# A 16-token opening, early branch constants, branch A's sums on DVE and a memory projection in single banks, in a one-core hybrid mixer layer

## The chip, the cores and the metric

The kernel is one program on 1 core of a Trainium2 chip. The core has TensorE (PE, with its weight loads PEld), VectorE (DVE), ScalarE (ACT), GpSimd (POOL), and SyncE (SP), which issues most of the transfers. The metric is the time of one execution in microseconds, as the device measures it; of several runs the median counts.

## What is computed

One layer, batch 1, for 1024 prompt tokens and 32 sample tokens, 1056 columns in all, width D = 1024, float32 (cut to what matters here):

```
h = rmsnorm(x, g_mix);  z = h @ w_in              # 1024 x 8192
qa fa va ga | xb gb | qc gc | za zb zc = split(z) # 4x512 | 2x1024 | 2x512 | 3x1024
pa = (rmsnorm(hgrn2(silu(qa), log f, 1-f, va)) * silu(ga)) @ w_a_down  # f = lb + (1-lb) sigmoid(fa)
pb = (lru_scan(conv4(xb)) * silu(gb)) @ w_b_down  # its gates use softplus(lambda) and biases
mk, mv = rmsnorm(mem, g_mem) @ w_mem_k, @ w_mem_v # 256 memory tokens x 512; both are outputs
pc = (softmax(qc mk^T / sqrt(128)) mv * silu(gc)) @ w_c_down   # the sample uses a cached mk, mv
y = rmsnorm(x + (sigmoid(za) pa + sigmoid(zb) pb + sigmoid(zc) pc) @ w_out, g_final)
```

## The kernel before, in words

**Products.** Every float32 matmul is three passes on a split of both operands: a rounded high part (`whi`, on ACT, L41) and the rest (`wlo`, on DVE, L44). The columns are cut into two halves of 528 tokens and the 1024 rows of `w_in` into two of 512. The input projection is done in a Strassen manner on these quarters: of the tokens the forms A11, A12, A22 and the sums S1 to S4 are held, and for every pair of 128-column blocks four sums of weight quarters are made (`sub`, L249, 128x512 each). A `slot(e)` is one such product, 24 matmuls of 264 columns into PSUM tiles X, V, Y or Z (L357 to L359). After its first half the slot lets waiting chains of small work go one step (`advance`), after the second half it runs also what is scheduled for it (`run_sched`: weight sums, and the weight split of a slot three later), and then `post` moves its results out of PSUM on DVE (u, L314; zh, L172) and ACT. Pairs come in this order: 3 pairs of merge-gate columns, then branch B mixed with gate pairs, then from pair `A_FROM` = 19 branch A and C, 13 pairs, whose sums go to POOL instead of DVE.

**Opening** (`ph0`). The tokens come in 10 chunks: chunks 0 to 4 of half one (the fifth has 16 tokens), 5 to 9 of half two; chunk c meets chunk 5+c in the sums. For a chunk: `n_load` (SP), `n_sq` (square on ACT, L405, then two small POOL operations for the root, L97/L98), `n_mul` (scaling by g_mix on DVE, L411), `put` (transposes on PE, L417, then the split on ACT and DVE). `sums(c)` makes S1 to S4 for a pair of chunks in four POOL operations (L428 to L431). `keep_warm` fills PE with transposes that nobody reads (L438). In between stand six first products (`pre`), whose results `pre_out` takes out through one buffer, pv, and stores.

**After the opening.** The chain `vec_consts` loads 9 small vectors and computes branch constants (gate bias, softplus of lambda, lb) during the first slots; its exponentials are at L584 to L586. Then come the slots of branches B and A; then 16 `mem_slot`s (six matmuls of 512 columns each into one two-bank tile psmem), between which the down projection of branch B (`bdown`, tile psdn, 9 matmuls of 384 columns for each of 8 inputs k) goes forward: it loads its inputs from DRAM (praw, SP), splits them into ph (ACT) and pl (DVE) in `prep_prods`. At its end `mem_slot` copies the result to om (ACT, L1024) and SP stores it twice, as output and, for the values, as vd (L1031). Attention of branch C, the other down projections and the output projection follow.

**PSUM.** `open_psum(na, nd)` closes the pools and opens others with other numbers of one-bank tiles (`abank`) and two-bank tiles (`dbank`); it is called before the slots, at A_FROM and twice around the memory stage. **Queues.** Each engine takes its instructions in the order in which they are written; SP's issues wait for the data that they store.

Of the kernel before, what the change touches and what calls it, by code (L numbers as in the profile page):

```python
# [7 lines left out]
F32 = mybir.dt.float32  # L8
# [7 lines left out]
D = 1024  # L16
# [16 lines left out]
def kernel(ctx: ExitStack, tc: tile.TileContext, I, O):  # L33
# [37 lines left out]
    def open_psum(na, nd, wide=True):  # L71
        if "st" in psum:
            psum["st"].close()
        st = psum["st"] = ExitStack()
        psum["a"] = st.enter_context(tc.tile_pool(name=f"aux{na}{nd}", bufs=na, space=PS))
        psum["d"] = st.enter_context(tc.tile_pool(name=f"dense{na}{nd}", bufs=nd, space=PS))

# [156 lines left out]
    def plan(p):  # L234
# [10 lines left out]

        eng = nc.gpsimd if p >= A_FROM else nc.vector

# [114 lines left out]
    def slot(e):  # L362
        p, k = ex[e]
        if "h" not in cur or cur["h"][0] != p:
            cur["h"] = (p, pairs[p][2]())
            if p < NPRE:
                cur["p1"] = plt.pop(p)
        form_, _, name = order(p)[k]
        new = (p, name) not in opened
        if new:  # L370
            opened.add((p, name))
            cur[name] = dbank(name)

        def after(q):
            advance(fast)
            advance(chains)
            if q == 1:
                run_sched(e)

        product(cur[name], wts.pop(e), form_, new, after)  # L380
        post(p, k, cur["h"][1])


# [4 lines left out]
    with tc.tile_pool(name="ph0", bufs=1, side="right", reuse_waits="tile") as ph0:  # L388
# [76 lines left out]

        n_load(0)
        nc.sync.dma_start(gx, bass.AP(tensor=I["g_mix"].tensor, offset=I["g_mix"].offset, ap=[[0, 128], [1, D]]))
        for s in range(1, 5):
            n_load(s)
        pre_load(0)  # L470
        for s in range(5, 8):
            n_load(s)
            pre_load(s - 4) if s < 7 else None
        keep_warm(30)
        n_sq(0)
        n_sq(1)
        n_mul(0)
        tt = {}
        for s in range(5):
            n_sq(s + 2)  # L480
            n_mul(s + 1)
            if s == 4:
                tt[0] = sums(0)
            keep_warm(6)
            put("A11", s, xts[s][:, 0:512])
            put("A12", s, xts[s][:, 512:D])
            if s >= 2:
                pre_hl(s - 2)
                pre_load(s + 1)
        run_sched(-8)  # L490
        n_load(8)
        n_sq(7)
        for c in range(5):
            if c < 4:
                n_mul(c + 6)
                tt[c + 1] = sums(c + 1)
            if c == 0:
                n_load(9)
            put("A22", c, xts[5 + c][:, 512:D])
            pre(c)  # L500
            if c:
                pre_out(c - 1)
            for x, name in zip(tt[c], ("S1", "S2", "S3", "S4")):
                put(name, c, x)
            if c < 2:
                n_sq(c + 8)
            if c < 3:
                pre_hl(c + 3)
# [6 lines left out]
        pre_out(4)  # L515
        run_sched(-2)
# [37 lines left out]

    def vec_consts():
        vt = T1("vt")[:NV, :128]
        for r, s in ((V_BCONV, I["b_conv"][0]), (V_BR, I["b_lru_r"][0]), (V_BI, I["b_lru_i"][0]),
                     (V_LAM, I["lru_lambda"][0]), (V_SL, I["state_lru"][0, 0]), (V_GA, I["g_a_out"][0])):
            nc.sync.dma_start(vt[r:r + s.shape[0] // 128, :], s.rearrange("(r c) -> r c", c=128))
        nc.sync.dma_start(vt[V_WC:V_WC + 32, :], I["w_conv"][0].rearrange("j (r c) -> (j r) c", c=128))  # L560
        nc.sync.dma_start(vt[V_SC:V_SC + 24, :], I["state_conv"][0, 0].rearrange("j (r c) -> (j r) c", c=128))
        nc.sync.dma_start(vt[V_LB:V_LB + 8, :], I["lb_logits"].rearrange("j (r c) -> (j r) c", c=128))
        gate_load(0)
        for _ in range(5):
            yield
        pt = abank("ptvec")
        nc.tensor.transpose(pt[:, :NV], vt, ident[:NV, :NV])
        nc.vector.tensor_copy(VT, pt[:, :NV])
        yield
        tq = T1("tq")  # L570
        lam = VT[:, V_LAM:V_LAM + 8]
        ab, e, q, q2, acc, mx = (tq[:, 8 * i:8 * i + 8] for i in range(6))
        l0, l1 = VT[:, V_LB:V_LB + 4], VT[:, V_LB + 4:V_LB + 8]
        t0, t1, m4 = (tq[:, 48 + 4 * i:52 + 4 * i] for i in range(3))
        nc.vector.tensor_scalar(ab, lam, -1.0, None, op0=OP.mult)
        nc.vector.tensor_scalar(mx, ab, 0.0, None, op0=OP.max)
        yield
        nc.vector.tensor_tensor(ab, ab, lam, op=OP.max)
        nc.vector.tensor_tensor(m4, l0, l1, op=OP.max)
        yield  # L580
        nc.vector.tensor_tensor(t0, l0, m4, op=OP.subtract)
        nc.vector.tensor_tensor(t1, l1, m4, op=OP.subtract)
        yield
        nc.scalar.activation(e, ab, AF.Exp, scale=-1.0)  # L584
        nc.scalar.activation(t0, t0, AF.Exp)
        nc.scalar.activation(t1, t1, AF.Exp)  # L586
        yield
        nc.vector.tensor_tensor(t1, t0, t1, op=OP.add)
        nc.vector.reciprocal(t1, t1)
        yield  # L590
        nc.vector.tensor_tensor(lb, t0, t1, op=OP.mult)
        nc.vector.tensor_scalar(oml, lb, -1.0, 1.0, op0=OP.mult, op1=OP.add)
        yield
        nc.vector.tensor_scalar(q, e, 2.0, None, op0=OP.add)
        nc.vector.reciprocal(q, q)
        yield
        nc.vector.tensor_tensor(q, q, e, op=OP.mult)
        nc.vector.tensor_tensor(q2, q, q, op=OP.mult)
        nc.vector.memset(acc, 1.0 / 15.0)
        for c in (13, 11, 9, 7, 5, 3, 1):  # L600
            nc.gpsimd.tensor_tensor(acc, acc, q2, op=OP.mult)
            nc.gpsimd.tensor_scalar(acc, acc, 1.0 / c, None, op0=OP.add)
        yield
        yield
        yield
        nc.vector.tensor_tensor(acc, acc, q, op=OP.mult)
        nc.vector.scalar_tensor_tensor(acc, acc, 2.0, mx, op0=OP.mult, op1=OP.add)
        nc.vector.tensor_scalar(spos, acc, 8.0, None, op0=OP.mult)
        nc.vector.tensor_scalar(sneg, acc, -8.0, None, op0=OP.mult)

    def mem_norm():
# [27 lines left out]

    chains.append(vec_consts())  # L640
    chains.append(mem_norm())
# [350 lines left out]
    def mem_k(om):  # L992
        for jj in range(2):
            pt = abank("ptk")
            for i in range(4):
                j, t = 2 * jj + i // 2, i % 2
                nc.tensor.transpose(pt[:, i * 128:(i + 1) * 128], om[:, t, j * 128:(j + 1) * 128], ident)
            yield
            kt = T1("kt")
            nc.vector.tensor_copy(kt[:, :512], pt)  # L1000
            for j in range(2):
                nc.sync.dma_start(ktd[2 * jj + j], kt[:, j * 256:(j + 1) * 256])
            yield
# [5 lines left out]
    def mem_slot(m):  # L1009
        mat, k = divmod(m, 8)  # L1010
        if k == 0:
            cur["M"] = dbank("psmem")
        wh, wl = (x.rearrange("p a c -> p (a c)") for x in wts.pop(NE + m))
        ks = slice(k * 128, (k + 1) * 128)
        for t in range(2):
            o = cur["M"][:, t, :]
            nc.tensor.matmul(o, memh[t][:, ks], wh, start=(k == 0), stop=False)  # L1017
# [22 lines left out]
    fstack.close()  # L1040
    open_psum(2, 3)

# [284 lines left out]
    pB, pA, pC = [], [], []  # L1327
    bprep = prep_prods(pbd, pB)
    bdown = down_steps("b", pB, 8, {6: lambda: late.append(prep_prods(pad, pA))}, 1.5)
    wload(0)  # L1330
    zload("b", 0)
    for m in range(16):
        mem_slot(m)
        if m in (0, 2, 4, 7, 9, 11):
            next(bprep)
        if m == 3:
            wprep(0)
        if m in (5, 7, 9, 11, 13):
            next(bdown)
# [156 lines left out]
```

## Time and profile before

| | |
|---|---|
| time, median of 3 runs | 1210.68 us (1206.56 to 1213.62) |
| the profiled execution: its time, its span | 1212.98 us, 1211.3 us |
| PE busy | 1139.2 us, 94% of the span |
| DVE, ACT, POOL busy | 735.7, 561.2, 251.0 us |
| granted TensorE clock, mean over the span | 0.976 of full speed |
| transfers | 130.11 MB, mean 107 GB/s |

The span runs from the first to the last instruction in the trace; the execution's own time is 1.7 us longer. A busy PE includes matmuls at a lower clock: PEclk 1.00 is 2.4 GHz and 0.50 is 1.2 GHz, and a mean between them is a stretch with both.

### The profile page before, as it was taken

The page shows a single profiled execution, that of the slowest core. Times are in us where ns is not written, and L with a number is a line of the kernel's source. Part 1 is how long each engine was busy: PE and PEld are TensorE (multiplying, and loading weights), DVE is VectorE, ACT ScalarE, POOL GpSimd, SP SyncE. Part 2 cuts the span into 40 slices and gives each one's busy share as a digit, 9 for nine tenths or more (in the row PEclk, how much of TensorE's full clock was granted, in tenths as well). Part 3 has the DMA queues.
Part 4 walks back from the last instruction along what each step waited for, and adds up shares of the span by engine and source line. Part 5 has one row for each costly group of instructions (what it writes and reads, how often), then busy time and mean ns, then how long its engine had stood idle before and what let it go on. Part 6 is the DMA issues. An engine that isn't in the chain of part 4 may idle for free. (4 is left out here: it accounts for less than half of the span.)

```text
span 1211.3 us, 21514 instructions
## 1 busy us (share of the span) xinstructions
PE 1139.2 (94%) x8350; PEld 1103.7 (91%) x8350; DVE 735.7 (61%) x1318; ACT 561.2 (46%) x1131; POOL 251.0 (21%) x396
## 2 busy tenths in 40 slices
PE   7788999999999999999998999998799999999998
PEld 6788999999999999998998999986699988899996
DVE  5745568668668668675555555655445577686222
ACT  5532465765765764653343534435423343343111
POOL 5801000000000002233323323220000014353111
PEclk8899999999999999999999999999899989899999
DMA  7163321321321321312203122138715344690321
GB/s 241 46 178 103 109 84 63 106 85 62 106 87 60 106 88 58 91 64 67 80 30 112 37 71 68 37 121 278 235 55 172 125 138 140 231 299 27 105 91 40
DMA packets 141705, 130.11 MB, mean 107 GB/s; under 512 B 10904, under 2 KB 122180, under 8 KB 141604
## 3 DMA queue, kind: packets, MB, share of 16 engines
q1 hardware_dynamic: 141604, 128.75, 33.6%
q8 instruction: 65, 1.06, 0.4%
q14 instruction: 36, 0.29, 0.1%
HBM read 93.93 MB, written 34.79 MB: 106 GB/s over the span
## 5 line engine op out<-in xcount | busy, mean ns | idle before, releaser
L44 DVE TENSOR_TENSOR wlo<-wraw,whi 128x512 fp32r<-128x512 f32 x208 | 156.2, 755 | 138.9 <-ACT whi L41 138.6
L41 ACT ACTIVATE whi<-wraw 128x512 fp32r<-128x512 f32 x208 | 126.4, 620 | 18.6 <-PE Z L358 6.6
L61 PE MATMUL psdn<-ph,whi 128*128 128x384 f32 (+1 forms) x384 | 128.6, 335 | 4.3 <-ACT whi L41 1.7
L61 PE MATMUL psdn<-pl,whi 128*128 128x384 f32 (+1 forms) x384 | 127.2, 331 | 4.9 <-DVE pl L44 4.9
L61 PE MATMUL psdn<-ph,wlo 128*128 128x384 f32 (+1 forms) x384 | 126.8, 330 | 0.3 <-DVE wlo L44 0.2
L357 PE MATMUL V<-S1h,whi 128*128 128x264 f32 x256 | 75.7, 296 | 10.6 <-DVE u L314 7.5
L61 PEld LDWEIGHTS psdn<-ph,whi 128*128 128x128 f32 x384 | 74.5, 194 | 6.9 <-ACT whi L41 2.1
L357 PE MATMUL X<-A11h,whi 128*128 128x264 f32 x256 | 76.1, 297 | 4.5 <-ACT pv L463 3.1
L61 PEld LDWEIGHTS psdn<-pl,whi 128*128 128x128 f32 x384 | 74.5, 194 | 5.4 <-DVE pl L44 5.2
L61 PEld LDWEIGHTS psdn<-ph,wlo 128*128 128x128 f32 x384 | 74.5, 194 | 1.1 <-DVE wlo L44 1.1
L44 DVE TENSOR_TENSOR wlo<-T,whi 128x512 fp32r<-128x512 f32 x64 | 44.6, 698 | 50.3 <-ACT whi L41 50.0
L359 PE MATMUL X<-A11h,wlo 128*128 128x264 f32 x256 | 74.8, 292 | 0.0
L358 PE MATMUL X<-A11l,whi 128*128 128x264 f32 x256 | 74.7, 292 | 0.0
L359 PE MATMUL V<-S1h,wlo 128*128 128x264 f32 x256 | 74.1, 289 | 0.0
L358 PE MATMUL V<-S1l,whi 128*128 128x264 f32 x256 | 73.8, 288 | 0.0
L357 PE MATMUL V<-S4h,whi 128*128 128x264 f32 x256 | 73.6, 287 | 0.0
L359 PE MATMUL V<-S4h,wlo 128*128 128x264 f32 x256 | 72.8, 284 | 0.0
L358 PE MATMUL V<-S4l,whi 128*128 128x264 f32 x256 | 72.7, 284 | 0.0
L61 PE MATMUL psout<-woh,mhi 128*128 128x384 f32 (+3 forms) x216 | 69.0, 319 | 0.1
L61 PE MATMUL psout<-woh,mlo 128*128 128x384 f32 (+3 forms) x216 | 68.8, 318 | 0.2 <-DVE mlo L44 0.2
L61 PE MATMUL psout<-wol,mhi 128*128 128x384 f32 (+3 forms) x216 | 68.8, 318 | 0.0
L174 ACT ACTIVATE zh<-zh 128x528 f32<-128x528 f32 x36 | 23.3, 646 | 96.6 <-DVE zh L172 55.4
(365 smaller groups left out, 3812.6 us busy)
## 6 DMA issues: line engine op xcount, KB each, us to landing
wraw<-in_w_in SPq DMA_DIRECT2D x134, 256.0 KB, 3.6
pbd<-sgb SPq DMA_DIRECT2D x8, 528.0 KB, 2.6
zda<-zh SPq DMA_DIRECT2D x16, 264.0 KB, 2.1
zdc<-zh SPq DMA_DIRECT2D x16, 264.0 KB, 2.5
wraw<-in_w_b_down SPq DMA_DIRECT2D x16, 256.0 KB, 5.2
xf<-in_x_prompt SPq DMA_DIRECT2D x8, 512.0 KB, 3.9
wraw<-in_w_out SPq DMA_DIRECT2D x16, 256.0 KB, 4.1
out<-xf SPq DMA_DIRECT2D x8, 512.0 KB
```

The lines of the kernel that those rows point to most:

```text
L41: nc.scalar.activation(out, in_, AF.Copy)
L44: (eng or nc.vector).tensor_tensor(out, a, hi.bitcast(F32), op=OP.subtract)
L61: nc.tensor.matmul(ps, a, b, start=st, stop=sp)
L174: nc.scalar.activation(t, t, self.act)
L357: nc.tensor.matmul(o, wh[:, i, :], fh[:, i, qs], start=bool(new) and i == 0, stop=False, **kw)
L358: nc.tensor.matmul(o, wh[:, i, :], fl[:, i, qs], start=False, stop=False, **kw)
L359: nc.tensor.matmul(o, wl[:, i, :], fh[:, i, qs], start=False, stop=(i == 3), **kw)
```

## The change

Five things are done at once.

1. **PSUM pools** are opened with `reuse_waits="tile"`: a tile of a new pool waits for the last use of its own banks, not for the whole pool before it. The second of the two `open_psum(2, 3)` calls (L1041) goes.
2. **Branch A's sums** (52 operations, 4 for each of 13 pairs) go from POOL to DVE, and in these pairs `run_sched(e)` comes after `post`.
3. **The opening** begins with the pair of 16-token chunks, 4 and 9, and has its sums (4) right behind; `five(c)` puts A22 and S1 to S4 of a pair, that of the 16 tokens behind chunk 1; `n_mul` of a chunk stands right before its `put`; there is less `keep_warm` (30 + 4x4 in place of 30 + 5x6), and `pre_out` follows its `pre` at once, one chunk earlier.
4. **The branch constants'** loads stand behind the loads of chunks 0 to 3, and seven of the chain's steps, the loads and the three exponentials among them, are taken in the opening; the others stay a chain.
5. **The memory stage:** psmem is two one-bank tiles, om is copied in two halves, the copy kt goes from DVE to ACT, and the stores of om, ktd and vd are issued from ACT. Branch B's loads run three inputs ahead, and the steps of `bprep` and `bdown` stand at other memory slots.

```
-        psum["a"] = st.enter_context(tc.tile_pool(name=f"aux{na}{nd}", bufs=na, space=PS))
+        psum["a"] = st.enter_context(tc.tile_pool(name=f"aux{na}{nd}", bufs=na, space=PS, reuse_waits="tile"))
...
-        eng = nc.gpsimd if p >= A_FROM else nc.vector
+        eng = nc.vector
...
-            if q == 1:
+            if q == 1 and p < A_FROM:
                 run_sched(e)
...
         post(p, k, cur["h"][1])
+        if p >= A_FROM:
+            run_sched(e)
...
+        for s in (4, 9, 0):
+            n_sq(s)
+        n_mul(4)
+        n_mul(9)
+        tt = {4: sums(4)}
...
+        put("A11", 4, xts[4][:, 0:512])
+        put("A12", 4, xts[4][:, 512:D])
+        n_load(7)
+        for s in range(4):
+            n_sq((1, 2, 3, 5)[s])
+            n_mul(s)
+            keep_warm(4)
             put("A11", s, xts[s][:, 0:512])
             put("A12", s, xts[s][:, 512:D])
+            if s:
+                pre_hl(s - 1)
+                pre_load(s + 2)
+            if s == 1:
+                five(4)
+                n_load(8)
+                next(vec)
+        n_sq(6)
+        n_mul(5)
+        tt[0] = sums(0)
...
+        pre(0)
+        pre_out(0)
+        pre_hl(3)
+        for c in range(4):
+            if c < 3:
                 tt[c + 1] = sums(c + 1)
+            put("A22", c, xts[5 + c][:, 512:D])
+            pre(c + 1)
+            pre_out(c + 1)
...
-            nc.vector.tensor_copy(kt[:, :512], pt)
+            nc.scalar.activation(kt[:, :512], pt, AF.Copy)
             for j in range(2):
-                nc.sync.dma_start(ktd[2 * jj + j], kt[:, j * 256:(j + 1) * 256])
+                nc.scalar.dma_start(ktd[2 * jj + j], kt[:, j * 256:(j + 1) * 256])
...
-            cur["M"] = dbank("psmem")
+            cur["M"] = [abank("psmem") for _ in range(2)]
...
-            nc.scalar.activation(om, cur["M"], AF.Copy)
             for t in range(2):
-                nc.sync.dma_start(O[5 + mat][0, 0, t * 128:(t + 1) * 128].rearrange("m j d -> m (j d)"), om[:, t, :])
+                nc.scalar.activation(om[:, t, :], cur["M"][t], AF.Copy)
+                nc.scalar.dma_start(O[5 + mat][0, 0, t * 128:(t + 1) * 128].rearrange("m j d -> m (j d)"), om[:, t, :])
...
-                    nc.sync.dma_start(vd[j], om[:, :, j * 128:(j + 1) * 128])
+                    nc.scalar.dma_start(vd[j], om[:, :, j * 128:(j + 1) * 128])
...
-    open_psum(2, 3)
...
-    bprep = prep_prods(pbd, pB)
+    bprep = prep_prods(pbd, pB, 3)
...
-        if m in (0, 2, 4, 7, 9, 11):
+        if m in (0, 5, 7, 9, 11, 13):
             next(bprep)
...
-        if m in (5, 7, 9, 11, 13):
+        if m in (8, 10, 12, 14, 15):
             next(bdown)
```

Three places show what the rewriting does to an engine's queue. The first is POOL in the opening. Before, all roots of chunks 0 to 6 (rsv, rsr) stand ahead of the first sums, which are those of chunk pair 0:

```order
L97 TENSOR_SCALAR rsv_323<-ss_321 128x1
L98 TENSOR_TENSOR rsr_324<-rsv_323,neghalf_66 128x1
L97 TENSOR_SCALAR rsv_356<-ss_354 128x1
L98 TENSOR_TENSOR rsr_357<-rsv_356,neghalf_66 128x1
L428 TENSOR_TENSOR sm_361<-xt_181 128x512
L429 TENSOR_TENSOR sm_362<-sm_361,xt_168 128x512
L430 TENSOR_TENSOR sm_363<-xt_168,xt_181 128x512
L431 TENSOR_TENSOR sm_364<-xt_168,sm_362 128x512
```

Now the roots of the 16-token chunks and of chunk 0 come first, then the four sums of the 16-token pair, and only then the root of chunk 1:

```order
L97 TENSOR_SCALAR rsv_239<-ss_237 16x1
L98 TENSOR_TENSOR rsr_240<-rsv_239,neghalf_66 16x1
L97 TENSOR_SCALAR rsv_245<-ss_243 128x1
L98 TENSOR_TENSOR rsr_246<-rsv_245,neghalf_66 128x1
L430 TENSOR_TENSOR sm_251<-xt_171 16x512
L431 TENSOR_TENSOR sm_252<-sm_251,xt_168 16x512
L432 TENSOR_TENSOR sm_253<-xt_168,xt_171 16x512
L433 TENSOR_TENSOR sm_254<-xt_168,sm_252 16x512
L97 TENSOR_SCALAR rsv_277<-ss_275 128x1
L98 TENSOR_TENSOR rsr_278<-rsv_277,neghalf_66 128x1
```

So every root from chunk 1 on stands behind four sums. The second place is DVE in branch A, where a slot of its first head ends; u is `post`'s, wlo the weight split, qr and sga belong to a head's chain. Before:

```order
L920 TENSOR_TENSOR R<-pu,S_6170 128x128
L952 SCALAR_TENSOR_TENSOR sga<-pot,VT,sga 128x384
L44 TENSOR_TENSOR wlo<-wraw,whi 128x512
L314 TENSOR_TENSOR u_6945<-Y,p_6870 128x528
L938 TENSOR_SCALAR qr<-po,rsr 32x128
L44 TENSOR_TENSOR wlo<-wraw,whi 128x512
L952 SCALAR_TENSOR_TENSOR sga<-pot,VT,sga 128x288
L44 TENSOR_TENSOR wlo<-wraw,whi 128x512
```

Now u stands ahead of the split, and the weight sums (L249) of a later pair stand in the same queue:

```order
L942 TENSOR_TENSOR R<-pu,S_6156 128x128
L974 SCALAR_TENSOR_TENSOR sga<-pot,VT,sga 128x384
L314 TENSOR_TENSOR u_6926<-Y,p_6852 128x528
L44 TENSOR_TENSOR wlo<-wraw,whi 128x512
L249 TENSOR_TENSOR wraw<-wraw,T_6566 128x512
L960 TENSOR_SCALAR qr<-po,rsr 32x128
L44 TENSOR_TENSOR wlo<-wraw,whi 128x512
L249 TENSOR_TENSOR T_6964<-wraw 128x512
L974 SCALAR_TENSOR_TENSOR sga<-pot,VT,sga 128x288
```

The split and the sums thus come behind the instruction that empties PSUM. The third place is ACT at the end of the memory projection (ph and whi are splits, om the copy of the last result). Before:

```order
L41 ACTIVATE ph<-praw 128x288
L41 ACTIVATE whi<-wraw 128x512 x3
L1024 ACTIVATE om<-psmem 128x1024
L41 ACTIVATE ph<-praw 128x384 x2
L41 ACTIVATE ph<-praw 128x288
L41 ACTIVATE ph<-praw 128x384 x2
L41 ACTIVATE ph<-praw 128x288
```

Now the copy is in two parts, and six DMA issues stand between it and the next splits:

```order
L41 ACTIVATE ph<-praw 128x288
L1047 ACTIVATE om<-psmem 128x512
L1048 DMA out<-om 128x512
L1047 ACTIVATE om<-psmem 128x512
L1048 DMA out<-om 128x512
L1053 DMA vd_80<-om 256x1x128
L1053 DMA vd_81<-om 256x1x128
L1053 DMA vd_82<-om 256x1x128
L1053 DMA vd_83<-om 256x1x128
L41 ACTIVATE whi<-wraw 128x512 x2
L41 ACTIVATE ph<-praw 128x384 x2
L41 ACTIVATE ph<-praw 128x288
```

The splits of the next two inputs (ph) and two weights wait behind these issues in ACT's queue.

## Rows read from the trace of the kernel before

**Rows 1.** The page, part 1: busy time of each engine, share of the span, instructions.
```profile
PE 1139.2 (94%) x8350; PEld 1103.7 (91%) x8350; DVE 735.7 (61%) x1318; ACT 561.2 (46%) x1131; POOL 251.0 (21%) x396
```

**Rows 2.** Waits of PE: us in total, times, longest us.
```profile
PE V L357 <- DVE u L314: 7.5, 9, 1.8
...
PE X L357 <- DVE u L314: 6.3, 3, 4.5
...
PE psdn L61 <- DVE pl L44: 4.9, 1, 4.9
...
PE psmem L1017 <- DVE zh L172: 3.4, 1, 3.4
...
PE X L357 <- DVE gb L655: 2.9, 7, 0.4
```

**Rows 3.** Windows: us, then PE, PEld, DVE, ACT, POOL, PEclk, DMA, GB/s.
```profile
68.00:72.00 4.00, 4.00 (x21) 4.00 (x22) 2.50 (x4) 1.53 (x3) 0.00 (x0) 0.58 0.49 144
...
84.00:88.00 4.00, 4.00 (x35) 4.00 (x34) 1.23 (x3) 2.71 (x6) 0.00 (x0) 1.00 0.76 224
...
96.00:100.00 4.00, 4.00 (x21) 4.00 (x22) 0.30 (x1) 0.00 (x0) 3.07 (x12) 0.58 0.22 60
...
826.00:832.00 6.00, 5.95 (x19) 4.76 (x20) 1.99 (x3) 2.30 (x4) 0.00 (x0) 0.72 0.56 177
...
832.00:836.00 4.00, 4.00 (x19) 3.06 (x17) 0.26 (x1) 0.81 (x2) 0.00 (x0) 1.00 1.03 337
```

**Rows 4.** Timeline of the opening: start, us, engine, line [idle before <- releaser].
```profile
4.27 1.06 ACT L405 ACTIVATE junk<-xt 128x1024 bf16<-128x1024 f32 x1 [2.20 <-DMA xt<-in_x_prompt]
...
5.78 0.56 POOL L98 TENSOR_TENSOR rsr<-rsv,neghalf 128x1 f32<-128x1 f32 x1
...
6.57 1.28 DVE L411 SCALAR_TENSOR_TENSOR xt<-xt,rsr,gx 128x1024 f32<-128x1024 f32 x1 [6.57 <-DMA gx<-in_g_mix]
...
7.97 1.06 ACT L405 ACTIVATE junk<-xt 128x1024 bf16<-128x1024 f32 x1 [2.55 <-DMA xt<-in_x_prompt]
...
22.51 2.82 POOL L428 TENSOR_TENSOR sm<-xt 128x512 f32<-128x512 f32 x1
...
28.08 1.91 PE L417 MATMUL pt<-ident,sm 128*128 128x128 f32 x16
...
29.35 0.69 DVE L44 TENSOR_TENSOR S1l<-pt,S1h 128x512 fp32r<-128x512 f32 x1 [4.56 <-ACT S1h L41]
...
58.27 1.28 POOL L431 TENSOR_TENSOR sm<-xt,sm 16x512 f32<-16x512 f32 x1
...
67.92 0.39 PE L357 MATMUL V<-S1h,whi 128*128 128x264 f32 x1 [3.14 <-ACT pv L463]
```

**Rows 5.** Timeline of ACT and PE around the branch constants.
```profile
84.52 1.28 ACT L584 ACT_TABLE_LOAD   x1
...
95.85 0.45 PE L357 MATMUL X<-S3h,whi 128*128 128x264 f32 x1 [4.47 <-DVE u L314]
```

**Rows 6.** Timeline of DVE and PE in branch A.
```profile
572.84 3.38 DVE L44 TENSOR_TENSOR wlo<-wraw,whi 128x512 fp32r<-128x512 f32 x1
...
576.99 0.36 PE L357 MATMUL V<-S1h,whi 128*128 128x264 f32 x1 [1.80 <-DVE u L314]
```

**Rows 7.** Groups of DVE, 130 to 460 us: count, busy us, mean ns, idle before.
```profile
L249 DVE TENSOR_TENSOR wraw<-wraw,T 128x512 f32<-128x512 f32 x15 | 10.3, 684 | 0.0
```

**Rows 8.** Timeline of ACT, SP, DVE and PE around the memory projection's end.
```profile
835.19 1.62 ACT L41 ACTIVATE ph<-praw 128x384 fp32r<-128x384 f32 x3 [5.88 <-DMA praw<-pbd]
...
861.22 1.02 ACT L1024 ACTIVATE om<-psmem 128x1024 f32<-128x1024 f32 x1 [3.62 <-PE psmem L1019]
...
863.14 2.62 SPq L1031 DMA_DIRECT2D vd<-om  x4
...
867.48 1.40 DVE L44 TENSOR_TENSOR pl<-praw,ph 128x384 fp32r<-128x384 f32 x3 [9.17 <-DMA vd<-om]
...
868.10 0.69 PE L61 MATMUL psdn<-pl,whi 128*128 128x384 f32 x1 [4.95 <-DVE pl L44]
```

More of the change, by code (lines that the diff above doesn't have):

```diff
@@ L74, in open_psum @@
         st = psum["st"] = ExitStack()
-        psum["a"] = st.enter_context(tc.tile_pool(name=f"aux{na}{nd}", bufs=na, space=PS))
-        psum["d"] = st.enter_context(tc.tile_pool(name=f"dense{na}{nd}", bufs=nd, space=PS))
+        psum["a"] = st.enter_context(tc.tile_pool(name=f"aux{na}{nd}", bufs=na, space=PS, reuse_waits="tile"))
+        psum["d"] = st.enter_context(tc.tile_pool(name=f"dense{na}{nd}", bufs=nd, space=PS, reuse_waits="tile"))
     def advance(lst):
@@ L467 @@
+        n_load(4)
         nc.sync.dma_start(gx, bass.AP(tensor=I["g_mix"].tensor, offset=I["g_mix"].offset, ap=[[0, 128], [1, D]]))
-        for s in range(1, 5):
+        n_load(9)
+        for s in (0, 1, 2, 3):
             n_load(s)
+        vec = vec_consts()
+        next(vec)
         pre_load(0)
-        for s in range(5, 8):
-            n_load(s)
-            pre_load(s - 4) if s < 7 else None
+        n_load(5)
+        pre_load(1)
+        n_load(6)
+        pre_load(2)
         keep_warm(30)
-        n_sq(0)
@@ L476, with five @@
[L476 to L484, printed above, removed]
+        for s in (4, 9, 0):
[3 more added lines that the diff above has]
+        tt = {4: sums(4)}
+        def five(c):
+            put("A22", c, xts[5 + c][:, 512:D])
+            for x, name in zip(tt[c], ("S1", "S2", "S3", "S4")):
+                put(name, c, x)
+        put("A11", 4, xts[4][:, 0:512])
@@ L485 @@
+        put("A12", 4, xts[4][:, 512:D])
[4 more added lines that the diff above has]
+            keep_warm(4)
             put("A11", s, xts[s][:, 0:512])
             put("A12", s, xts[s][:, 512:D])
-            if s >= 2:
-                pre_hl(s - 2)
-                pre_load(s + 1)
+            if s:
[4 more added lines that the diff above has]
+                n_load(8)
+                next(vec)
@@ L490 @@
+        n_sq(6)
+        n_mul(5)
+        tt[0] = sums(0)
         run_sched(-8)
-        n_load(8)
         n_sq(7)
-        for c in range(5):
-            if c < 4:
-                n_mul(c + 6)
+        n_mul(6)
+        next(vec)
+        pre(0)
[3 more added lines that the diff above has]
+            if c < 3:
                 tt[c + 1] = sums(c + 1)
+            put("A22", c, xts[5 + c][:, 512:D])
+            pre(c + 1)
+            pre_out(c + 1)
             if c == 0:
[L498 to L502, printed above, removed]
+                n_sq(8)
+            if c < 2:
+                n_mul(c + 7)
@@ L503 @@
             for x, name in zip(tt[c], ("S1", "S2", "S3", "S4")):
                 put(name, c, x)
+            next(vec)
             if c < 2:
-                n_sq(c + 8)
-            if c < 3:
-                pre_hl(c + 3)
+                pre_hl(c + 4)
             if c == 1:
@@ L514 @@
         run_sched(-3)
-        pre_out(4)
         run_sched(-2)
@@ L553, in gate_load @@
                     nc.sync.dma_start(graw[s, t, s], I[nm][0, 2 * i + b])
[L555 to L609, printed above, removed]
@@ L638, in mem_norm @@
             yield
-    chains.append(vec_consts())
+    gate_load(0)
+    chains.append(vec)
     chains.append(mem_norm())
@@ L1015, in mem_slot @@
         for t in range(2):
-            o = cur["M"][:, t, :]
+            o = cur["M"][t]
             nc.tensor.matmul(o, memh[t][:, ks], wh, start=(k == 0), stop=False)
@@ L1102, in split_prod, with prep_prods @@
         return h, l
-    def prep_prods(srcs, out):
-        nxt = load_prod(srcs[0])
+    def prep_prods(srcs, out, ahead=1):
+        nxt = [load_prod(x) for x in srcs[:ahead]]
         for i in range(len(srcs)):
-            raw = nxt
             yield
-            if i + 1 < len(srcs):
-                nxt = load_prod(srcs[i + 1])
-            out.append(split_prod(raw))
+            if i + ahead < len(srcs):
+                nxt.append(load_prod(srcs[i + ahead]))
+            out.append(split_prod(nxt.pop(0)))
     merged = [[None] * 3 for _ in range(8)]
```

54 lines of the change are left out of this document (53 added, 1 removed).

## The prediction

> **What bounds the kernel now.** The page first: PE is busy for 94% of the span [rows 1], so time is lost only in short gaps of PE, and in what follows them. The list of waits, with PE as the waiting engine, names the gaps: DVE's u before V and X, pl before psdn, zh before psmem [rows 2]. The windows then show a second price: after a gap the granted clock falls. In 84 to 88 us PE runs 35 matmuls at clock 1.00, 0.114 us each; in 68 to 72 and 96 to 100 only 21, at 0.58 [rows 3]. Fourteen matmuls short, at 0.114: such a stretch costs 1.6 us on top of the gap. In 826 to 832 the clock is 0.72, and 6 x 0.28 = 1.7 us are lost [rows 3]. Last come the timelines of the four places which the change touches: opening, constants, branch A, end of the memory projection [rows 4 to 6, 8]. DVE at 61% and POOL at 21% are no bound over the span; each is one in a stretch.
>
> **Opening.** The mark is the matmul at 67.92 us, with which the first slot begins [rows 4]. Before, POOL's sums of pair 0 start at 22.51 [rows 4], and five rounds follow, to 59.55 (58.27 + 1.28), 7.4 us each. Four sums take 2.82 + 3 x 1.28 = 6.7 us, so POOL is about the pace of a round. From 59.55 to 67.92 come transposes, the last first product and, at its end, 3.14 us of waiting for pv.
>
> After the change I lay the chain out anew. Two transfers of 512 KB part the two squares at 4.27 and 7.97, so one takes 1.85; g_mix now goes ahead of chunk 0, whose square begins at about 6.7 (it needs the two 16-token chunks too) and whose root is done at 8.9 (square 1.06, small operations, 0.56). Then the order shows POOL taking the four sums of the 16-token pair. A 16x512 sum took 1.28 at 58.27, as long as one of 128 rows; I take 6.7 for the four (bounds 5.1 and 6.7), so to 15.5, and chunk 1's root comes at 16.4. From there n_mul, transposes, and two splits of a chunk stand in a row: 1.28 for n_mul (at 6.57), 1.4 from the transposes' start to the second half of the first split's end (28.08 to 29.35 and a little), and 3 x 0.6 for what the splits still need, 4.5 in all. Chunks 1 to 3 are 13.5, the 16-token pair's five splits in between about 2.5, n_mul of chunk 5 1.3: pair 0's sums start at about 34, 11.5 us later than before. But only four rounds are left. With 6.9 each (bounds: 6.0, where sums overlap, and the old 7.4) they end at 61.6. The transposes of the last S (sixteen took 1.91 [rows 4], so 0.6 for four with their start), the last product of 24 x 0.114 = 2.7 and 0.7 for its weights give 65.6. That is 2.3 us earlier; since pv is emptied a step sooner, I also take the low stretch of 68 to 72 as gone, 1.6. **Term: 3.9**, bounds -4 (rounds of 7.4, the 16-token pair in the way of chunks 1 to 3, and ACT's two table loads of 1.28 [rows 5], which now fall among the splits) and +8.5 (POOL's short sums and rounds of 6.0). keep_warm's fewer transposes cost nothing while PE waits for data.
>
> **Branch constants.** At 84.52 ACT loads a table for the exponentials [rows 5], DVE then waits for ACT's weight splits, and PE's wait for u follows at 95.85, 4.47 long. The other two waits of this sort make (6.3 - 4.47) / 2 = 0.9 each [rows 2]. I take 0.9 as what stays: 3.6, and 1.6 for the clock of 96 to 100. **Term: 5.2**, bounds 2 (the last steps of the chain still stand in the first slots, where DVE can wait for POOL's fourteen small operations) and 6. The 9 small loads now stand on SP ahead of the first weight blocks; these are wanted only after the splits of chunk 0, and are covered by POOL's lateness above.
>
> **Branch A.** At 572.84 a weight split takes 3.38 us on DVE in place of the usual 0.7, u stands behind it, and V waits 1.80 [rows 6]. Of the nine such waits three are of this size and the others near 0.3 [rows 2]; with u ahead of the split 3 x 1.5 = 4.5 go. On the other side 52 sums come to DVE at 0.684 [rows 7], 35.6 us spread over some 350. In branch B, where DVE has had the sums, X waits 7 times 0.4 for DVE's gb [rows 2]; for four heads I take 4 x 0.4 = 1.6. **Term: 2.9**, bounds -3 (every pair waits once for 0.6) and 8 (small roots on POOL come sooner and shorten the heads' chains as well). POOL's release counts for nothing elsewhere.
>
> The long split overlaps POOL's sums, which read the same memory. The Trainium skill ("SBUF — State Buffer", Who interferes with whom) says that VectorE's second port pair is shared with GpSimd under an exclusive lock; the one row here agrees with it (3.38 against 0.7). By that rule DVE's splits in branch A should all fall back to 0.69, and the 1.6 charged above would fall away: 4.5 in place of 2.9.
>
> **Memory stage.** PE waits 3.4 for zh before the first psmem [rows 2], since the new pool waits for all banks of the old. By tile, the two banks that psmem takes were free earlier, and the memory rows' last split limits it: 1.0 left, 2.4 gained. The low clock of 826 to 832 goes with it: 1.7 [rows 3]. In the middle ACT stands 5.88 for praw [rows 8], which keeps weights from PE; with loads three ahead these come sooner. PE ran through most of it, though (4.00 of 4 in 832 to 836 [rows 3]), so I take 0.7, nearer to nothing than to half of the 5.88. At the end, the last memory product is done at 861.2 (om starts at 861.22), and PE gets at k = 5 in earnest at 868.10, after waiting 4.95 for pl, whose DVE instruction had stood 9.17 for the vd stores [rows 8]: 6.9 us. After the change ACT must first do two halves of om (1.1), six issues and then two weights (1.1) and a first ph (0.45). Four issues on SP took 2.62, 0.65 each [rows 8], and I take as much for ACT, which shows none: 3.9. So k = 5 comes 6.6 us after the last memory product: 0.3 gained. But k = 4, nine matmuls of 384 columns, now lies inside this gap and not ahead of it: 9 x 0.21 x 384/512 = 1.4 (0.21 is 4.00 over 19 in the 832 window, mostly of 512 columns). End: 1.7, bounds -2 (an issue costs double) and 5.6 (it costs nothing on ACT). **Term: 6.5**, bounds 0 and 12.7 (the middle at 3, the end at 5.6).
>
> The pools' other switch, at the first A slot, and one pool fewer: 0 (at most 1.5), since only waits of a few tenths show there.
>
> **Sum.** 3.9 + 5.2 + 2.9 + 6.5 = 18.5. The profiled execution took 1212.98 (span 1211.3 and 1.7 around it), 2.3 more than the median of 1210.68; from the one it leads to 1194.5, from the other to 1192.2. I predict **1192 us**.
>
> **Rivals.**
> *The memory stage is bound by its transfers (1197, 0.15).* In 832 to 836 the DMA share is 1.03 at 337 GB/s [rows 3]: the rings are full. Loads three ahead only ask sooner for what comes no sooner, and an input that is late for one slot costs what the wait before it gave. Then 2.4 and 1.7 stay less a new idle of 2, and the end gives nothing: about 2 of 6.5. Against it: PE was busy for all of these 4 us. Beside the row: the Trainium skill ("DMA: Bandwidth & Descriptors", Issuing engines are not separate DMA queues) says that issuing from several engines saves only the time on the sequencer; the row agrees, and by it the six stores on ACT free SP and not the rings.
> *The opening is cheaper (1187, 0.13).* Short sums of 1.28 each and rounds of 6.0: slot 0 at about 61, 4.6 sooner.
> *The opening is dearer (1200, 0.13).* Rounds of 7.4 or more with the table loads among them: slot 0 at about 72, the low clock stays (6.4 + 1.6).
> *Reuse by tile does nothing (1196, 0.05).* If the banks that psmem takes are those of the last zh, the 3.4 and its clock stay: 4 less.
> *Slower: DVE becomes the pace of branch A (1226, 0.04).* Each sum on the path costs 0.684; all 52 make 35.6, and the term turns from 2.9 to 4.5 - 35.6 = -31. 27 of them on the path (18.5 / 0.684) use up all the other gains. Against it: DVE is busy for 61% [rows 1], and where it had the sums already PE waited 0.4 a pair.
> For the forecast itself, 0.5.
>
> **Range and chances.** The forecast's own spread is 1186 to 1199 (the bounds of single terms, not all at one end). With both rivals of the opening and the transfers' rival inside, 1178 to 1203 leaves out the slower case and the far ends of the opening and of ACT's issues, some 2 in 10. A measurement of this kernel tells 0.5%, 6 us, from no change: below 1204.6 is faster, above 1216.7 slower. The forecast and the rivals of 1187 to 1200 lie below; from their upper ends I take 0.09 for the middle, and with it 0.04 for the rival of branch A and 0.02 for an opening later by over 10 us still: faster 0.85, same 0.09, slower 0.06.
>
> **What would show it.** Opening: the sums of pair 0 on POOL at 34, not 22.5, and slot 0's first matmul near 66. Constants: no wait of X for u over 1 us and clock 1.00 between 60 and 130. Branch A: V's waits for u below 3 us in all, the splits near 0.7, and no wait of PE for a split. Memory: psmem's first wait near 1, pl no longer behind vd, and k = 5 about 6.6 us after the last memory product. It is wrong if roots come so late that slot 0 starts after 72, if DVE's idle in branch A vanishes, or if PE stands for praw between the memory slots.

## The result and the profile after

The changed kernel takes 1192.97 us (median of 4 runs, 1191.04 to 1195.18) against 1211.7 us (4 runs, 1206.56 to 1213.62): ratio 0.9853, 95% interval 0.9817 to 0.9888. The forecast was 1192 us and the range 1178 to 1203. Total and direction were right; three of the four terms behind them were not. Marks (the starts of the same matmul in the two profiled executions, us) show it:

| stretch, and the mark at its end | before | after | gained in it | predicted |
|---|---|---|---|---|
| opening: first slot (V from S1) | 67.92 | 69.84 | -1.9 | 3.9 (with the low clock behind it) |
| constants: a slot after the old stall (V from S4) | 100.37 | 99.34 | 3.0 | 5.2 |
| rest of branch B and first slots of A: V from S1 | 542.20 | 540.36 | 0.8 | 0 |
| branch A: the last such V | 810.15 | 794.93 | 13.4 | 2.9 |
| memory stage, psdn after its wait for sz | 876.37 | 860.42 | 0.7 | 6.5 |
| to the end: span | 1211.3 | 1191.6 | 3.7 | 0 |

Branch A gave 10 us more than its term, the opening and the memory stage nearly 12 less, and 3.7 came in a stretch which the change hardly touches. PE's waits after (us in total, times, longest) answer to [rows 2]:

```profile
PE pt L419 <- DVE xt L413: 11.3, 5, 4.2
...
PE ptk L1019 <- ACT om L1047: 5.6, 2, 5.0
...
PE psdn L61 <- ACT ph L41: 4.2, 1, 4.2
...
PE X L357 <- DVE u L314: 3.8, 3, 2.0
...
PE X L357 <- DVE gb L677: 2.9, 7, 0.4
...
PE pot L969 <- DVE qr L960: 1.5, 4, 0.4
...
PE psdn L61 <- DVE pl L44: 0.2, 1, 0.2
```
The waits of V for u and of psmem for zh, 7.5 and 3.4 before, are gone, and that for pl is 0.2. The waits for scaled tokens in the opening grew to 11.3 (6.1 in five waits before), and in the memory stage PE now waits 5.0 for om and 4.2 for ph (1.5 before). The windows there answer to [rows 3] (columns as there):

```profile
816.00:820.00 4.00, 4.00 (x19) 3.16 (x18) 1.96 (x4) 1.79 (x3) 0.00 (x0) 1.00 1.05 358
...
820.00:824.00 4.00, 1.51 (x7) 0.83 (x5) 2.02 (x4) 1.36 (x3) 0.00 (x0) 0.95 1.03 355
...
824.00:828.00 4.00, 0.88 (x3) 0.58 (x4) 1.39 (x2) 2.37 (x5) 0.00 (x0) 0.50 1.06 359
...
828.00:832.00 4.00, 4.00 (x18) 3.62 (x17) 1.39 (x3) 1.99 (x5) 0.00 (x0) 0.70 1.03 374
```
The low clock that stood at 826 to 832 before is still here, behind another gap: PE is busy 1.51 and 0.88 of 4 us, while the transfers run at a share of 1.03 to 1.06.

### The profile page after: what moved, and what is told of

Its sections match the earlier page's. It is cut to its first block, busy times and chain, and to the rows that moved or that the text cites. A ratio compares the mean times of both kernels' runs of the same rounds, so it can differ in the third digit from the quotient of the medians.

```text
span 1191.6 us, 21456 instructions
## 1 busy us (share of the span) xinstructions
PE 1131.2 (95%) x8336; PEld 1096.4 (92%) x8336; DVE 746.0 (63%) x1368; ACT 562.3 (47%) x1135; POOL 178.7 (15%) x344
## 3 DMA queue, kind: packets, MB, share of 16 engines
q8 instruction: 65, 1.06, 0.4%
## 5 line engine op out<-in xcount | busy, mean ns | idle before, releaser
L44 DVE TENSOR_TENSOR wlo<-wraw,whi 128x512 fp32r<-128x512 f32 x208 | 145.1, 702 | 134.8 <-ACT whi L41 134.3
```

The source lines that it names most:

```text
L44: (eng or nc.vector).tensor_tensor(out, a, hi.bitcast(F32), op=OP.subtract)
```

## The experiments

Each kernel is the one before or the changed one with the edit shown; "before" was timed again beside them, 1209.71 to 1211.68. The times of the variants are medians of 2 to 8 runs. What a single stage does is read from marks in the trace.

**Branch A: the sums, the order, or both.** First the sums alone, on the kernel before:

```
-        eng = nc.gpsimd if p >= A_FROM else nc.vector
+        eng = nc.vector
```


> The kernel before with one change: branch A's 52 weight sums on DVE, everything else in its old order. In the changed kernel, branch A (from the slot at 549 us to the first memory product) came 14 us nearer. Theory 'shared memory port': POOL's sums stretch DVE's splits (3.38 us in place of 0.7), so moving the sums alone removes the stretch and gives at least 8 of the 14 us; the time is near 1202 us. Theory 'order': u still stands behind a split and, now, behind a sum too; the waits of V for u stay near 1 us and the move alone gives under 4 us, or costs some; the time is 1208 to 1214 us.

Measured 1201.5 us (3 runs; ratio 0.9913, 0.987 to 0.9956). Then the order alone, on the kernel before:

```
-            if q == 1:
+            if q == 1 and p < A_FROM:
                 run_sched(e)
...
         post(p, k, cur["h"][1])
+        if p >= A_FROM:
+            run_sched(e)
```


> The kernel before with one change: in branch A's pairs the scheduled work stands behind the instructions that empty PSUM, the sums stay on POOL. Theory 'order': u no longer waits for a stretched split, V's waits for u fall from 7.5 us to under 2, and at least 8 of branch A's 14 us are gained; the time is near 1202 us. Theory 'shared memory port': some split still takes over 3 us and what stands behind it (the heads' qr and sga) still comes late; under 4 us are gained.

Measured 1196.48 us (2 runs; 0.9874, 0.9825 to 0.9923): one edit gives more than three quarters of what the whole change does. Between the V marks at 542.20 and 810.15 above, branch A is 14.7 us shorter than before; with the sums alone it is 8.8. Of the changed kernel the table has 13.4 there, since about 1 us of its gain lies ahead of the first of these marks: from the last V of branch B (464.51 before) to the last slot (819.58) it gains 14.5, the order alone 14.7 and the sums alone 9.0. Here is the group of weight splits on DVE, in 470 to 800 us, with the order alone and in the changed kernel (count, busy us, mean ns):

```profile
L44 DVE TENSOR_TENSOR wlo<-wraw,whi 128x512 fp32r<-128x512 f32 x67 | 60.2, 899 | 24.9 <-ACT whi L41 24.9
```
```profile
L44 DVE TENSOR_TENSOR wlo<-wraw,whi 128x512 fp32r<-128x512 f32 x67 | 46.0, 686 | 29.1 <-ACT whi L41 28.9
```
With the order alone the splits are still stretched, 899 ns on average against 686, more than the 818 of the kernel before, and PE does not wait for it. PE's waits in branch A (530 to 805 us) with the sums alone, and then with the order alone:

```profile
PE pot L947 <- DVE qr L938: 4.0, 4, 1.0
...
PE pu L909 <- ACT kt L902: 1.6, 4, 0.4
```
```profile
PE V L357 <- DVE u L314: 1.8, 4, 1.0
...
PE pot L949 <- DVE qr L940: 0.2, 1, 0.2
```
Sums on DVE take away V's waits (6.5 us in this window before) but not those of pot and pu, 4.0 and 1.6 as before; the order shortens all three to 2.0 together. So a head takes 74.0 us with the order alone, read from its V rows:

```profile
543.27 0.36 PE L357 MATMUL V<-S1h,whi 128*128 128x264 f32 x1 [0.95 <-DVE u L314]
...
617.31 0.36 PE L357 MATMUL V<-S1h,whi 128*128 128x264 f32 x1 [0.28 <-DVE u L314]
...
691.34 0.36 PE L357 MATMUL V<-S1h,whi 128*128 128x264 f32 x1 [0.28 <-DVE u L314]
```
(before, from 576.99 [rows 6] to 656.11 and on to 733.75: 79.1 and 77.6). The changed kernel has the same 74.0, from the first rows of pot of its heads:

```profile
561.17 0.55 PE L969 MATMUL pot<-ident,qr 128*128 128x128 f32 x3 [0.40 <-DVE qr L960]
...
635.18 0.55 PE L969 MATMUL pot<-ident,qr 128*128 128x128 f32 x3 [0.40 <-DVE qr L960]
...
709.18 0.55 PE L969 MATMUL pot<-ident,qr 128*128 128x128 f32 x3 [0.38 <-DVE qr L960]
```
The last question is whether the sums' move does anything once the order is there. The changed kernel with the sums on POOL again (`eng` as before):

> The changed kernel with branch A's sums back on POOL, the new order kept. Theory 'order' (from the run in which the order alone gave 14.8 us and from a pace of 74.0 us a head both there and in the changed kernel): nothing is lost, the time is within 3 us of the changed kernel's 1193, a head still takes 74 us, though some splits on DVE take over 3 us again. Theory 'both are needed': the heads get slower by 1 us or more each and the time is near 1198.

Measured 1194.21 us (2 runs; 0.9868, 0.9806 to 0.9929), the same as 1192.97 within the spread, with the splits at 899 ns and 74.0 us a head; between the same two marks it gains 14.8. The theory "order" stands, and "both are needed" falls. Either edit alone relieves DVE's queue, the order wholly and the sums in part; together they give no more than the order.

**The opening.** The new opening and the early constants alone on the kernel before (those hunks of the diff):

> The kernel before with the new opening and the early branch constants alone. The changed kernel's first slot began at 69.84 us, 1.9 later than before, and by the slot after the old constants' stall it was 1.0 earlier. If the parts add up, this kernel shows the same two marks (first slot at 69.8, then 1 to 2 us ahead) and ends 1 to 2 us earlier than before, near 1209.5. The prediction's term (3.9 for the opening and 5.2 for the constants) would make it 9 us earlier, near 1201.5.

Measured 1211.13 us (8 runs; 1.0, 0.9979 to 1.0021). The first slot begins at 69.81, and at the slot after the old stall the kernel is 2.6 ahead; of this 0.8 is left at the last V of branch A, and the first memory product is 0.4 late. Two places give it back. From 652 to 660 us, behind V's wait for u, the clock is 0.77 and 0.81 where it was 1.00 before, and 1.5 us of the lead go; and the first memory product waits 4.68 for zh in place of 3.40. Here is what the changed kernel's opening does on POOL, from its timeline:

```profile
14.95 1.26 POOL L433 TENSOR_TENSOR sm<-xt,sm 16x512 f32<-16x512 f32 x1
...
16.57 0.56 POOL L98 TENSOR_TENSOR rsr<-rsv,neghalf 128x1 f32<-128x1 f32 x1
...
36.73 1.28 POOL L430 TENSOR_TENSOR sm<-xt 128x512 f32<-128x512 f32 x1
...
62.85 1.31 POOL L433 TENSOR_TENSOR sm<-xt,sm 128x512 f32<-128x512 f32 x1
```
and on DVE, `n_mul` of chunks 1, 2, 3 and 5:

```profile
17.17 1.28 DVE L413 SCALAR_TENSOR_TENSOR xt<-xt,rsr,gx 128x1024 f32<-128x1024 f32 x1 [1.16 <-POOL rsr L98]
...
24.39 1.27 DVE L413 SCALAR_TENSOR_TENSOR xt<-xt,rsr,gx 128x1024 f32<-128x1024 f32 x1
...
29.62 1.28 DVE L413 SCALAR_TENSOR_TENSOR xt<-xt,rsr,gx 128x1024 f32<-128x1024 f32 x1
...
34.80 1.28 DVE L413 SCALAR_TENSOR_TENSOR xt<-xt,rsr,gx 128x1024 f32<-128x1024 f32 x1
```
Chunk 1's root comes at 17.1 (16.4 predicted), a chunk takes 5.2 us (4.5 predicted), the sums of pair 0 start at 36.73 (34). The four rounds took (64.16 - 36.73) / 4 = 6.9, as predicted. The 0.7 that a chunk takes longer is the clock: it is 0.50 from 12 to 32 us (0.83 over the same 20 us before). Chunk 3's eight transposes take 1.97 there. In the kernel with the opening alone the clock is back by then, and they take 1.09:

```profile
30.96 1.97 PE L419 MATMUL pt<-ident,xt 128*128 128x128 f32 x8 [2.35 <-DVE xt L413]
```
```profile
31.41 1.09 PE L417 MATMUL pt<-ident,xt 128*128 128x128 f32 x8 [2.35 <-DVE xt L411]
```
In this second kernel chunk 3 takes 34.53 - 30.07 = 4.5 us, read from `n_mul`:

```profile
30.07 1.28 DVE L411 SCALAR_TENSOR_TENSOR xt<-xt,rsr,gx 128x1024 f32<-128x1024 f32 x1
...
34.53 1.28 DVE L411 SCALAR_TENSOR_TENSOR xt<-xt,rsr,gx 128x1024 f32<-128x1024 f32 x1
```
Whether the fewer `keep_warm` transposes or PE's longer waits for the chunks brought the clock down is not shown: no run has the old `keep_warm` in the new opening. To part POOL's queue from the chain of chunks, the roots were moved ahead of the sums:

```
-        for s in (4, 9, 0):
+        for s in (4, 9, 0, 1, 2, 3):
             n_sq(s)
...
-            n_sq((1, 2, 3, 5)[s])
+            if s == 3:
+                n_sq(5)
             n_mul(s)
```


> The changed kernel with the squares and roots of chunks 1 to 3 ahead of the 16-token pair's four sums. Theory 'POOL's queue': the root of chunk 1, at 17.1 us because it stood behind the sums, comes near 12, the sums of pair 0 start 4 us sooner than 36.7, and the first slot begins near 66; time near 1189. Theory 'serial chunks': DVE's chain n_mul, transposes, splits sets the pace whatever the roots do; the sums of pair 0 start less than 1.5 us sooner and the first slot stays near 69.

Measured 1193.02 us (2 runs; 0.9858, 0.9807 to 0.9909): nothing. Its `n_mul` of chunks 0, 1, 2, 3 and 5 stand here on DVE:

```profile
12.89 1.28 DVE L413 SCALAR_TENSOR_TENSOR xt<-xt,rsr,gx 128x1024 f32<-128x1024 f32 x1
...
17.47 1.47 DVE L413 SCALAR_TENSOR_TENSOR xt<-xt,rsr,gx 128x1024 f32<-128x1024 f32 x1
...
24.88 1.28 DVE L413 SCALAR_TENSOR_TENSOR xt<-xt,rsr,gx 128x1024 f32<-128x1024 f32 x1
...
30.11 1.28 DVE L413 SCALAR_TENSOR_TENSOR xt<-xt,rsr,gx 128x1024 f32<-128x1024 f32 x1
...
35.29 1.28 DVE L413 SCALAR_TENSOR_TENSOR xt<-xt,rsr,gx 128x1024 f32<-128x1024 f32 x1
```
The root of chunk 1 now comes early, but three squares on ACT stand ahead of the splits of the 16-token chunk, `n_mul` of chunk 0 starts 2.5 later for it (12.89 against 10.37), that of chunk 1 at 17.47, and the rest keeps its pace of 5.2. My theory "POOL's queue" falls for this edit; the chain of n_mul, transposes and splits sets the time, here too at clock 0.50.

**PSUM and the memory stage.** Reuse by tile alone, all pool switches kept (`reuse_waits="tile"` in `open_psum` of the kernel before):

> The kernel before with the PSUM pools' reuse by tile alone, all pool switches kept. The prediction's step: the wait of 3.4 us for zh ahead of the first memory product goes (to about 1, for the memory rows' split) with the low clock behind it, 3 to 4 us in all, time near 1207.5. Rival: psmem's banks are those of the last zh, so the wait stays and the time is 1211.

Measured 1211.34 us (8 runs; 0.9984, 0.9961 to 1.0007). Neither side was right: the wait goes, and the time stays. PE's timeline:

```profile
825.08 0.51 PE L1017 MATMUL psmem<-whi,mh 128*128 128x512 f32 x1 [0.52 <-ACT mh L41]
...
838.54 0.69 PE L61 MATMUL psdn<-ph,whi 128*128 128x384 f32 x1 [4.70 <-ACT whi L41]
```
0.52 stands where 3.40 did, and 4.70 for a weight split where it was 1.69 before: the first k of the down projection starts at 838.5 against 837.9. Reuse by tile did one more thing, in the old opening: the wait of 3.14 for pv at the first slot is gone, and the first slot starts at 64.50 (66.64 to 67.92 in the four kernels with this opening and the old pools, each with 2.8 to 3.3 of that wait). The next two waits of X for u take it back (2.65 and 6.70 us, before 0.89 and 4.47), and at the slot after the old stall 0.8 of the 3.4 is left. The stage's parts without the other three changes, on the kernel before:

> The kernel before with the memory stage's part alone (single banks, copies and stores on ACT, loads three ahead, steps at other slots, one PSUM pool fewer). The prediction's term says 6.5 us earlier, near 1204.5. What the two traces say: the wait of 3.4 us at its start goes, and 2.9 us are lost in the middle (PE waits 5.0 us for om behind a weight split that waits for its load); so about 0.8 us earlier up to the end of the stage, and 1 to 3.5 us earlier in all, if the low-clock stretch in the attention stage goes as well.

Measured 1210.44 us (8 runs; 0.9984, 0.9971 to 0.9998): 0.9 us by the medians, 1.9 by the ratio, with an interval of 0.2 to 3.5. It has both new waits of the changed kernel, 5.21 for om and 4.21 for ph. Where they come from, ACT's waits in the changed kernel show (814 to 853 us):

```profile
ACT whi L41 <- DMA wraw<-in_w_mem_v: 3.3, 2, 3.0
...
ACT whi L41 <- DMA vd<-om: 3.1, 1, 3.1
```
om stands in ACT's queue behind a split whose weight lands 3.0 late. So om and its stores went ahead of that split (in the changed kernel; the last slot calls `run_sched(NE + m)` behind the copies):

> The changed kernel with the copy of the memory product (om, its stores) ahead of the weight split that the last slot of each half schedules. Theory 'ACT's queue': PE's wait of 5.0 us for om goes to under 1.5, with the low clock behind it (824 to 832), so 4 to 6 us are gained and the time is near 1188. Theory 'the loads': the weight's transfer, behind nine loads of 1.6 MB, sets the pace all the same; PE waits for the next memory slot's weights in place of om and under 2 us are gained.

Measured 1192.28 us (2 runs; 0.9852, 0.9796 to 0.9907). PE still waits 4.18 for om, since the split of the slot before waits for its weight too (3.35). The theory "the loads" stands. Nine loads, 1.6 MB together, are issued ahead of most of those weights; with one input ahead (`prep_prods(pbd, pB, 1)`) and with two:

> The changed kernel with branch B's loads one input ahead, as in the kernel before, in place of three (nine transfers of 1.6 MB at the first memory slot become three). Theory 'the loads': the nine transfers push back the value weights, so the split that ACT's queue waits for (3.0 us) and with it om and PE (5.0 us) come sooner; PE's wait for om goes under 2 us, and the stage ends 3 to 5 us sooner, time near 1189. Theory 'the stage is bound by its bytes': the same 9 MB have to come, the idle time moves to the inputs' splits (PE waiting for ph or whi), and the time stays within 2 us of 1193.

> The same with two inputs ahead. Theory 'the loads': the wait for om is between the other two, time near 1191. Theory 'the stage is bound by its bytes': within 2 us of 1193.

Measured 1189.37 us (2 runs; 0.9826, 0.9797 to 0.9854) and 1191.7 us (2 runs; 0.9845, 0.9816 to 0.9874). PE's wait for om is 2.32 and 3.86, against 5.04 with three; the order of loads is its main cause. The gain is smaller than the 3 to 5 expected: from the first memory product to the stage's last mark (psdn after sz), one input ahead gains 2.0 us on the changed kernel, two lose 0.1 and om's place alone gains 0.8. Behind that mark the last two lose about 1 us again, in stretches of low clock (near 958 and 1000 us) which the changed kernel's trace does not have. What else these three have of a lead is from the first 110 us, where the code is the same. Then the stores from SP again (`nc.sync.dma_start` for out, ktd and vd, all else as changed):

> The changed kernel with the stores of om, kt and vd issued from SP again. The prediction's step: ACT loses six issues of 0.34 to 0.65 us, 3.3 in all, between the last memory product and k = 5, so PE's wait of 4.2 us for ph falls to about 1 and 2 to 3 us are gained, unless pl stands behind the vd stores again. Rival: with SP issuing, the loads behind the stores come later (SP waits for om), PE's wait for ph or pl stays near 4, and the time is 1192 to 1196.

Measured **1187.1 us** (2 runs, 1186.37 and 1187.84; 0.9807, 0.9779 to 0.9836), the lowest median here, though its interval overlaps with that of one input ahead. PE's wait for ph at k = 5 and the windows behind it:

```profile
847.65 0.44 PE L61 MATMUL psdn<-ph,whi 128*128 128x384 f32 x1 [0.68 <-ACT ph L41]
```
```profile
844.00:848.00 4.00, 3.32 (x17) 2.66 (x16) 1.30 (x3) 3.05 (x7) 0.00 (x0) 1.00 0.41 146
...
848.00:852.00 4.00, 3.57 (x21) 3.30 (x21) 3.62 (x9) 2.67 (x8) 0.00 (x0) 1.00 0.74 209
...
852.00:856.00 4.00, 2.92 (x18) 2.69 (x17) 2.97 (x7) 1.26 (x2) 0.00 (x0) 1.00 0.99 279
```
The wait is 0.68 in place of 4.19, and the clock stays at 1.00, where the changed kernel has 0.50 in 852 to 856. The marks agree: the lead over the changed kernel grows from 0.6 us at the last memory product to 6.2 at the stage's last mark, and 5.5 are left at the end. The vd stores no longer hold ACT, and PE's wait for pl is 0.43. At last all three edits together:

> The changed kernel with three edits of its memory stage: stores from SP, branch B's loads one input ahead, om's copy ahead of the split scheduled in the same slot. If the gains add (5.5 us in the trace for the stores, about 2 for the loads once the earlier arrival of the other marks is taken off, up to 1 for the copy), PE's waits in the stage are under 2.5 for om and under 1 for ph, the time is near 1184. If the stage is bound by its bytes, one of the gains is given back as a wait for loads, and the time stays at the 1187 of the stores alone.

Measured 1190.04 us (5 runs, 1189.29 to 1194.59; 0.9842, 0.9819 to 0.9865): the gains do not add. Here are SP's issues, then ACT's wait:

```profile
837.95 1.70 SPq L1049 DMA_DIRECT2D out<-om  x2
...
839.71 2.59 SPq L1054 DMA_DIRECT2D vd<-om  x4
...
843.60 2.87 SPq L1117 DMA_DIRECT2D praw<-pbd  x6
```
```profile
848.10 1.31 ACT L41 ACTIVATE ph<-praw 128x384 fp32r<-128x384 f32 x3 [7.29 <-DMA praw<-pbd]
```
PE's wait for om is 1.28, and at the last memory product PE is 7.5 us ahead of the last variant (2.4 of it from before the stage), but with one input ahead the last two inputs are issued at 843.60, behind the six stores, and ACT waits 7.29 for them. All of the lead is lost in this one place. So stores from SP go with loads three ahead. With loads one ahead and the stores on ACT, PE's wait for ph is 4.28. Stores from SP with om first and three ahead were not tried.

## Why the prediction came out, step by step

**Opening (3.9; measured -1.9).** The layout was right in kind: POOL's sums of the 16-token pair ahead of the roots, four rounds of 6.9, no wait for pv. Three sizes were off. A chunk's chain takes 5.2, not 4.5, since I had priced its transposes at full clock; my line that fewer `keep_warm` transposes cost nothing left the clock out, and it was 0.50. With the later root (0.7) the sums start 2.7 late. And behind the last sums I took four transposes (0.6), but all sixteen of the last pair's S1 to S4 come there, so the last product starts at 66.83, 2.7 after the sums' end and not 1.3. Together 4.2 us (69.84 against 65.6). The rival "dearer" (slot 0 at 72) was nearer than the forecast, though not for its reasons: the rounds were not longer. The root as the cause was not shown: moving it changed nothing. Nor is the missing wait for pv due to the opening alone: the old opening loses it by reuse of PSUM by tile, and the new one without that reuse still waits 0.85 for it.

**Constants (5.2; measured 3.0).** X's wait of 4.47 at 95.85 [rows 5] is 0.89 now, as assumed, and 5.2 us are gained from the V of 79.46 (83.62 after) to that of 100.37 (99.34). But ahead of it PE waits 0.89 for a weight split at 71.22 and 2.02 for u at 79.09, where 0.89 stood, and the low clock of 68 to 72, which I had booked as gone, came at 80 to 84 (0.64). These early marks also differ from run to run: the first transposes of the memory rows come at 109.5 in the changed kernel, at 106.8 to 111.0 in six kernels with the same opening, and at 110.6 before. At the mark of 99.34, the changed kernel and the two of these that have the low clock near 80 stand at 99.0 to 100.8, the other four at 96.6 to 97.0. So opening and constants together gained between -0.4 and 3.7 us on the kernel before, where 9.1 were forecast; the table's 1.0 is one case of it.

**Branch A (2.9; measured 13.4).** This is the step that failed most: its sum left out most of the waits, and a low clock, that the new order takes away. I priced the three long waits of V and charged 1.6 for DVE's extra work. The trace before had 6.5 us of V's waits between 530 and 805, all of which went; 4.0 of pot's for qr and 1.6 of pu's (shown above, with the sums alone), which I had put into the upper bound only or not at all (1.5 and 0.4 are left); and a low clock of 0.66 behind the wait at 576.99, 1.4 us in 576 to 580, of the sort that I had priced everywhere else:

```profile
PE V L357 <- DVE u L314: 6.5, 7, 1.8
```
```profile
576.00:580.00 4.00, 3.02 (x14) 2.81 (x14) 1.90 (x4) 0.86 (x2) 3.07 (x3) 0.66 0.01 4
```
With 0.5 of Z's wait for ga, these are 6.5 + 2.5 + 1.2 + 0.5 + 1.4 = 12.1 of 13.4. The charge for DVE did not come: PE waits for DVE in no new place, though 52 sums more stand there, and with the sums back on POOL the stretch is only 0.3 shorter (14.8 gained against 14.5).

The Trainium skill ("SBUF — State Buffer", Who interferes with whom) says that VectorE's second port pair is shared with GpSimd under an exclusive lock. The runs agree on the stretch: 899 ns with sums on POOL, 686 without. They show as well that the stretch had a price only while u stood behind the split. By that rule, I had written, the term would be 4.5 in place of 2.9, and that too was short by two thirds.

**Memory (6.5; measured 0.7).** The wait for zh went as said: the first memory product gains 3.6 on the last slot, where I had 2.4. The step that failed is the middle, priced at 0.7 and 1.7 for its clock: from the first memory product to the end of the last, the stage takes 38.9 us (807.17 to 846.10) in place of 35.1, a loss of 3.8. The rival "bound by its transfers" (about 2 of 6.5) is the case, or worse. What I had called a risk at the end only (praw between the slots) cost 5.0 for om, through ACT's queue. The end gained 0.9 where I had 1.7: k = 5 came 851.75 - 846.10 = 5.7 us after the last memory product, against 6.6 predicted, so the sum of ACT's copies, issues and splits was near (the six issues took 3.3, not 3.9). But the wait for pl did not need the issues on ACT: with stores on SP and loads three ahead it is 0.43, and with loads one ahead a wait behind the stores returns (6.16 for ph). The loads' distance is a cure by itself, and the issues on ACT cost 5 us. The Trainium skill ("DMA: Bandwidth & Descriptors", Issuing engines are not separate DMA queues) says that issuing from several engines saves sequencer time alone; here that time went over to ACT's queue, where splits that PE needs stand behind it: the issues took 3.3 us, and the 3.1 that the next weight split waits behind vd, shown above, are the last five of them.

**The rest (0; measured 3.7).** Some 2.5 to 3 of it are a stretch at clock 0.58 and 0.57 (976 to 984 us before), behind PE's wait for qh at the first scores of the third head of attention; in the changed kernel the clock there is 1.00:

```profile
976.00:980.00 4.00, 3.04 (x12) 2.77 (x13) 3.28 (x8) 1.81 (x5) 0.21 (x1) 0.58 0.73 230
```
The run with the memory part alone still has it, and the runs with the opening alone, with two inputs ahead and with all three edits have half of it; the others have not. The waits ahead of it overlap in length (1.10 to 2.05 with the low clock, 1.17 to 1.89 without). What decides it stays open.

So the forecast of 1192 was right by luck, as a sum in which +10.5 and +3.7 from two places made up for -5.8, -5.8 and -2.2 from three others; the range owed its success to this, not to its bounds: one term lay outside its own and one near the edge (13.4 over 8, and 0.7 of 0 to 12.7).

## What to carry to other kernels

When an engine's queue is late, ask first what stands ahead of the instruction that the bottleneck waits for; putting the release of PSUM ahead of prepared work gave more than moving 52 operations to another engine. In a stage whose transfers run at full share, a wait that is taken away can come back at the next load in the queue (2.9 us came back as 3.0 here), so read the gain at the stage's last mark and not at the wait. A total that fits proves none of its terms: compare marks of the same instruction stage by stage.

## What the runs showed of the hardware

DMA issues on ACT took as long as on SP (four for vd: 2.61 us on ACT, 2.62 on SP). On POOL a sum of 16x512 took as long as one of 128x512 (1.25 to 1.28 us for most), so 16 partitions in place of 128 saved nothing here. Eight transposes of 128x128 took 1.97 us at clock 0.50 and 1.09 at 1.00. A gap of PE did not always bring a low clock: 0.58 followed 2.05 and 0.66 us of waiting in one run, 0.68 followed 1.10 and 0.57 in a second, and 1.00 followed 1.89 and 0.57 in a third.
